# A build-time timetable that learns of the port shared by VectorE and GpSimd, takes its durations from a trace, and may send more elementwise operations to VectorE

## The chip, the core and the metric

The kernel runs on one core of a Trainium2 chip. The core has a matrix engine (PE, TensorE), an engine for elementwise work with two tensor inputs (DVE, VectorE), one for activations with scale and bias (ACT, ScalarE), a general engine (POOL, GpSimd) and a queue that issues DMAs (SP, SyncE). The engines run their own instruction streams in order and wait for each other by semaphores. The metric is the device time of one execution in microseconds (us); lower is better.

## What is computed

Two layers of a diffusion backbone over 512 latent tokens and 256 context tokens, width 1024, all in float32. Layer 0 mixes tokens with gated linear attention (GLA, 4 heads) and differential attention (4 heads) side by side; layer 1 with a bidirectional state-space mixer (SSD, 32 heads in 8 groups of 4). Each layer then runs a SwiGLU feed-forward network (FFN) of hidden width 2816. In short:

```
for layer in range(DEPTH):
    mod_x = jax.nn.silu(c) @ mod_w[layer] + mod_b[layer]          # 6 shifts, scales, gates
    hx = x * (1.0 + scm_x) + shm_x                                 # the same for ctx with mod_c
    if layer % 2 == 0: mix_c, mix_x = even_mixer(hc, hx, ...)      # GLA and differential attention
    else:              mix_c, mix_x = odd_mixer(hc, hx, ...)       # SSD
    x = layer_norm(ALPHA * x + gm_x * mix_x, ln_g[layer, 0], ln_b[layer, 0])
    x = layer_norm(ALPHA * x + gf_x * swiglu(x * (1.0 + scf_x) + shf_x, ...), ln_g[layer, 1], ln_b[layer, 1])
    # ctx goes through the same norms, gates and FFN in layer 0
```

## The kernel before

Activations stay in SBUF, tokens in 6 tiles of 128. Weights stream from HBM into 3 slots (`RAW`, 128x1024). Every float32 product is made of three passes (`mm3`): each operand is split into a rounded high part (`hi`, made by ScalarE as a Copy into an fp32r tile) and a low part (`lo = x - hi`, a two-input subtraction on VectorE or GpSimd). For weights that is `RW<-RAW` and `RW<-RAW,RW` in `issue_loads`; for FFN activations `f<-HB` and `f<-HB,f`; for a layer's normed input `R<-HX,R` (shown by the order of instructions as `R_69`).

The kernel is written as one recording pass. `mm`, `dma`, and the proxies `V`, `S`, `G` (VectorE, ScalarE, GpSimd) do not emit an instruction at once: the class `Timing` gives each one a start in a timetable (`fit`, `room`: the first gap on its engine after its inputs are ready) and `flush` emits them all in the order of those starts. So the timetable's costs decide the order on every engine. Work beside the weight products (softmax steps of differential attention, GLA's recurrences, the SSD tiles, the LayerNorm chains) is written as generators (`Chain`); `pump` lets a chain take its next step between two products when the timetable's PE clock has come to the time at which that step's inputs are ready. So the costs also decide where a chain's matmuls stand among the weight products on PE.

`Timing.either` chooses VectorE or GpSimd for a two-input operation: VectorE, if its end plus a bias (in us, given by the caller) is not later than GpSimd's end. Before, the biases are 0 to 9.5, in GpSimd's favour, and a dozen call sites name GpSimd outright: the rotary products in `diff_proj`, `att`, `la`, the gate and residual of `LN.prep` and `LN.finish`, the sums of `y_tile`, the recurrence product of `recur`, half of `mod_sums`. The power in a normalisation (`ALU.pow` with `mhalf`: `sml<-sml,mhalf`, `LNS<-LNS,mhalf`, `RS<-RS,mhalf`) always runs on GpSimd.

In differential attention a unit (one head, one token tile, 24 in all) is a chain: scores on PE, `TENSOR_REDUCE sml<-PS` for the maximum, `sml` scaled, exponentials on ACT, reciprocal, `HB<-HB,sml` 128x768 to combine the two maps, transposes, values, and a tail whose norm goes through GpSimd's power and ends in `TENSOR_SCALAR HB<-HB,sml` 128x128. In layer 1, `conv_out` (`HB<-HB,CW`, 128x770) makes the convolution and each `y_tile` (32 of them) an output tile. `mod_sums` (layer 1's modulation, made during layer 0's FFN) scales rows of `mod_w` and adds them up.

Names in rows: HB is the large buffer of work units, PS is PSUM, R and HX the mixer's input and its float32 form, RAW and RW weights, f FFN slots, l mixer slots, sml, LNS, RS, DS and CBD small statistics. L104 (L105 after) is the line of `flush` that emits everything, so rows are told apart by their tiles.

## Time and profile before

| what | before |
| --- | --- |
| time, median of 3 runs | 2091.33 us (2087.03 to 2094.28) |
| the profiled execution | 2081.43 us, of which the span of the trace is 2079.5 us |
| PE busy | 1935.3 us (93%) |
| DVE, ACT, POOL busy | 1167.9, 809.5, 1037.8 us (56%, 39%, 50%) |
| chain that ended last | PE 57%, DVE 24%, POOL 6%, ACT 6%, issue 5%, DMA 2% |

Busy time of PE is that of pipelined matmuls whose ends are modelled, so it overstates how full PE is. The chain that ended last is followed back from the last instruction: at each step to what released it, or to the instruction before it on its engine.

### The profile page before, as it was taken

To read this page: it belongs to the slowest core of one execution; us is meant where nothing else is said; L and a number is where in the kernel's file an instruction comes from. 1 tells how busy PE (TensorE), PEld (TensorE's weight loads), DVE (VectorE), ACT (ScalarE), POOL (GpSimd) and SP (SyncE) were. 2 spreads that over 40 slices of the span, in tenths; PEclk is the share of its full clock that TensorE was granted. 3 is DMA by queue.
4 is the path that set the end of the run, shared out by engine and by line. 5 is a ranking of instruction groups with operands and counts; after the bars stand their busy time and mean duration, and the time that the engine had idled before them with its cause. 6 is when DMAs were issued, how large, how long until landed. Compare 5 with 4: busy or idle time off the path is not lost.

```text
span 2079.5 us, 27508 instructions
## 1 busy us (share of the span) xinstructions
PE 1935.3 (93%) x10660; PEld 1655.0 (80%) x10660; DVE 1167.9 (56%) x1660; ACT 809.5 (39%) x1512; POOL 1037.8 (50%) x714
## 2 busy tenths in 40 slices
PE   7988999988899999999998888999999889999997
PEld 4867687866799999999886777888787678888885
DVE  3564535478631424423348998877868883223237
ACT  3523135434524333334235355554545443222232
POOL 2423142335774666657587455541725766333355
PEclk9999899998999999999999999999999999999998
DMA  8443411112243443434422423222233324333331
GB/s 277 122 135 104 132 41 30 43 59 75 70 147 108 123 141 112 142 123 124 150 87 61 130 72 101 92 75 89 82 111 102 111 92 146 108 101 100 103 101 61
DMA packets 233360, 217.43 MB, mean 105 GB/s; under 512 B 18901, under 2 KB 202839, under 8 KB 233231
## 3 DMA queue, kind: packets, MB, share of 16 engines
q1 hardware_dynamic: 233231, 215.69, 33.9%
q8 instruction: 83, 1.36, 0.3%
q14 instruction: 46, 0.38, 0.1%
HBM read 204.94 MB, written 10.72 MB: 104 GB/s over the span
## 4 chain that ended last, share of the span: by engine, by line
PE 57%; DVE 24%; POOL 6%; ACT 6%; issue 5%; DMA 2%; SPq 0%; POOLq 0%; ACTq 0%; DVEq 0%
PE PS L104 57%; DVE HB L104 14%; POOL HB L104 5%; ACT HB L104 4%; DVE RW L104 2%; DVE l L104 2%; DVE sml L104 2%; DVE HX L104 1%; DVE LNS L104 1%; ACT RW L104 1%; DVE R L104 1%; DMA HB<-in_x_dram 0%; DMA HB<-acs_rows 0%; ACT R L104 0%; POOL R L104 0%
## 5 line engine op out<-in xcount | busy, mean ns | idle before, releaser
L104 PE MATMUL PS<-R,RW 128*128 128x384 f32 (+3 forms) x5184 | 989.6, 349 | 10.2 <-DVE R L104 4.2
L104 PEld LDWEIGHTS PS<-R,RW 128*128 128x128 f32 (+1 forms) x5184 | 888.0, 189 | 94.9 <-issue 15.5
L104 POOL TENSOR_TENSOR HB<-HB 128x256 f32<-128x256 f32 (+3 forms) x262 | 441.0, 1694 | 183.3 <-ACT HB L104 105.6
L104 POOL TENSOR_TENSOR RW<-RAW,RW 128x1024 fp32r<-128x1024 f32 (+1 forms) x135 | 340.0, 2525 | 332.4 <-ACT RW L104 325.3
L104 PE MATMUL PS<-RW,f 128*128 128x512 f32 x1320 | 307.1, 392 | 6.1 <-DVE RW L104 4.7
L104 ACT ACTIVATE RW<-RAW 128x1024 fp32r<-128x1024 f32 (+1 forms) x222 | 229.3, 1047 | 213.6 <-issue 100.6
L104 PEld LDWEIGHTS PS<-RW,f 128*128 128x128 f32 x1320 | 248.1, 189 | 60.1 <-DVE RW L104 5.8
L104 ACT ACTIVATE HB<-PS 128x512 f32<-128x512 f32 (+4 forms) x247 | 129.5, 533 | 417.8 <-PE PS L104 408.8
L104 DVE TENSOR_TENSOR HB<-HB,PS 128x384 f32<-128x384 f32 (+2 forms) x68 | 39.7, 584 | 358.4 <-PE PS L104 358.0
L104 DVE TENSOR_TENSOR HB<-PS,HB 128x512 f32<-128x512 f32 (+2 forms) x276 | 160.1, 587 | 143.4 <-PE PS L104 120.6
L104 DVE TENSOR_TENSOR RW<-RAW,RW 128x1024 fp32r<-128x1024 f32 x87 | 167.8, 1931 | 88.4 <-ACT RW L104 86.9
L104 ACT ACTIVATE HB<-HB 128x128 f32<-128x128 f32 (+4 forms) x372 | 160.6, 490 | 138.0 <-DVE HB L104 111.2
L104 PE MATMUL PS<-RW,R 128*128 128x256 f32 (+1 forms) x1440 | 199.0, 296 | 8.5 <-ACT R L104 4.2
L104 PEld LDWEIGHTS PS<-RW,R 128*128 128x128 f32 x1440 | 184.7, 194 | 16.8 <-ACT R L104 4.6
L104 PE MATMUL PS<-HB 128*128 128x128 f32 (+6 forms) x896 | 154.7, 362 | 26.2 <-DVE HB L104 12.5
L104 PE MATMUL PS<-RW,l 128*128 128x512 f32 x576 | 156.0, 417 | 6.3 <-DVE l L104 1.9
L104 PEld LDWEIGHTS PS<-HB 128*128 128x128 f32 (+3 forms) x896 | 106.0, 194 | 60.2 <-issue 23.3
L104 POOL TENSOR_TENSOR f<-HB,f 128x384 fp32r<-128x384 f32 (+2 forms) x63 | 88.8, 1410 | 122.8 <-ACT f L104 122.7
L104 PEld LDWEIGHTS PS<-RW,l 128*128 128x128 f32 x576 | 108.4, 195 | 34.0 <-DVE l L104 2.6
L104 PE MATMUL PS<-ident,HB 128*128 128x128 f32 x480 | 79.7, 295 | 54.4 <-DVE HB L104 36.9
L104 PEld LDWEIGHTS PS<-ident,HB 128*128 128x128 f32 x480 | 57.3, 149 | 85.1 <-DVE HB L104 38.3
L104 DVE SCALAR_TENSOR_TENSOR HB<-HB,CW 128x770 f32<-128x770 f32 (+1 forms) x96 | 104.5, 1088 | 2.8
(145 smaller groups left out, 1471.1 us busy)
## 6 DMA issues: line engine op xcount, KB each, us to landing
RAW<-in_ffn_w_in_dram SPq DMA_DIRECT2D x88, 512.0 KB
HB<-in_mod_w_dram SPq DMA_DIRECT2D x48, 512.0 KB
RAW<-in_ffn_w_out_dram SPq DMA_DIRECT2D x44, 512.0 KB
RAW<-in_ssd_w_in_dram SPq DMA_DIRECT2D x40, 512.0 KB
mod<-in_mod_w_dram SPq DMA_DIRECT2D x72, 256.0 KB
HB<-acs_rows SPq DMA_DIRECT2D x64, 256.0 KB
RAW<-in_ev_w_in_dram SPq DMA_DIRECT2D x20, 512.0 KB
xres<-HB SPq DMA_DIRECT2D x16, 512.0 KB
```

The source lines that it names most:

```text
L104: f(*a, **k)
```

## The change

Three things. First, the timetable's costs: other fixed and per-element numbers for VectorE (V), ScalarE (S) and GpSimd (G), for the power, for scans, and for matmuls. Second, a resource L: an operation that reads two SBUF tensors on VectorE, a VectorE `tensor_scalar` or `tensor_copy` from SBUF, and everything but a memset on GpSimd now also books L, so that the timetable places no two such operations at the same time on the two engines. Third, the choice: the biases are gone, GpSimd is taken only if it would end earlier than VectorE by more than the difference of the two costs, the sites that named GpSimd go through `either`, and in `mod_sums` the second half of the products (an ACT scale and a POOL add each) becomes the fused VectorE operation of the first half.

```
@@ COST and busy
-        "V": (0.069, 1.042e-3, 0.03, 0.06),
-        "S": (0.09, 0.833e-3, 0.06, 0.09),
-        "G": (0.13, 2.12e-3, 0.0, 0.0),
+        "V": (0.15, 1.06e-3, 0.03, 0.06),
+        "S": (0.16, 0.875e-3, 0.08, 0.19),
+        "G": (0.16, 2.14e-3, 0.0, 0.0),
...
-        self.busy = {e: [] for e in "VSGQD"}
+        self.busy = {e: [] for e in "VSGQDL"}
@@ product
-        cost = self.gated(t, cost + 0.0027)
+        cost = self.gated(t, cost)
@@ engine
+                    wide = [x for x, m in zip(aps[1:], sizes[1:]) if x not in out and (m > 1 or n == 1)]
+                    lock = op != "memset" if name == "G" else len(wide) > 1 and self.locks(*wide)
                     if ALU.pow in a:
-                        cost = 0.3 + 0.165 * n
+                        cost = 0.38 + 0.165 * n
...
-                        cost = fixed + 0.66e-3 * n
+                        cost, lock = fixed + 0.64e-3 * n, n > 1
+                    elif op == "tensor_tensor_scan":
+                        cost = fixed + 2.1e-3 * n
...
-                    t = self.fit(name, t, cost)
+                    t = self.fit(name, t, cost, lock)
@@ either
-    def either(self, out, a, b, op, bias=0.0):
+    def locks(self, *ins):
+        return all(x.space != bass.MemoryType.PSUM for x in ins)
+
+    def either(self, out, a, b, op):
...
-        (self.V if end["V"] + bias <= end["G"] else self.G).tensor_tensor(out, a, b, op)
+            end[e] = self.room(e, max(t, self.floor.get(e, 0.0)), cost[e], lock or e == "G") + cost[e]
+        g = end["G"] + cost["G"] - cost["V"] < end["V"]
+        (self.G if g else self.V).tensor_tensor(out, a, b, op)
@@ room and fit (the old room is now gap)
+    def room(self, name, t, cost, lock=False):
+        while True:
+            t0, t = t, self.gap(name, t, cost)[0]
+            if lock:
+                t = self.gap("L", t, cost)[0]
+            if t == t0:
+                return t
@@ mm
-        tm.product(o, (l, r), (max(n, 2 * m) if l.dtype == F32R else 4 * max(n, m)) / 2400.0,
+        tm.product(o, (l, r), max(n, 2 * m) / 2400.0 + 0.0133 if l.dtype == F32R else 4 * max(n, m) / 2400.0 + 0.005,
@@ issue_loads
-            tm.either(lo, r, hf, ALU.subtract, 2.0 if limit < len(plan) else 1 if plan[j][0][0] in ("cv", "z", "sw") else 2)
+            tm.either(lo, r, hf, ALU.subtract)
@@ mod_sums
-                    elif m == 0:
+                    else:
                         V.scalar_tensor_tensor(a, r, c, a, ALU.mult, ALU.add)
-                    else:
-                        S.activation(r, r, AF.Copy, scale=c)
-                        G.tensor_tensor(a, a, r, ALU.add)
@@ LN.prep (LN.finish, gate, gla_mix, diff_proj and start likewise)
-            G.tensor_tensor(y, y, self.gate[1 if t < 2 else 0], ALU.mult)
-            G.tensor_tensor(y, y, xr, ALU.add)
+            tm.either(y, y, self.gate[1 if t < 2 else 0], ALU.mult)
+            tm.either(y, y, xr, ALU.add)
@@ LN.chain and gated
-                tm.either(R0[:, 1, ks, c], hx[:, ks, :], R0f[:, 0, ks, c], ALU.subtract, 0.0 if quick else 9.5)
+                tm.either(R0[:, 1, ks, c], hx[:, ks, :], R0f[:, 0, ks, c], ALU.subtract)
...
-                tm.either(RA[c % 5][:, 1, cs], h, RAf[c % 5][:, 0, cs], ALU.subtract, 6.5)
+                tm.either(RA[c % 5][:, 1, cs], h, RAf[c % 5][:, 0, cs], ALU.subtract)
@@ recur and y_tile
-                G.tensor_tensor(heads(s2), heads(s), dv, ALU.mult)
+                tm.either(heads(s2), heads(s), dv, ALU.mult)
...
-            G.tensor_tensor(tt, tt, yo[:, 0:256], ALU.add)
-            G.tensor_tensor(tt, tt, yo[:, 256:512], ALU.add)
+            tm.either(tt, tt, yo[:, 0:256], ALU.add)
+            tm.either(tt, tt, yo[:, 256:512], ALU.add)
```

What it makes of the built program, counted over all its instructions: the matmuls (9886) and the DMAs stay the same in number. GpSimd goes from 719 to 283 instructions, VectorE from 1654 to 2090, ScalarE from 1410 to 1368 (the 42 scalings of `mod_sums`). The largest kinds:

| operation | on GpSimd, before / after | on VectorE, before / after |
| --- | --- | --- |
| weight low part `RW<-RAW,RW` 128x1024 | 133 / 23 | 87 / 197 |
| `HB<-HB` 128x1024 (LN gates, residuals, gains; `mod_sums`) | 114 / 18 | 0 / 54 |
| `HB<-HB` 128x256 (`y_tile`, `recur`) | 128 / 36 | 0 / 92 |
| `HB<-HB,HX` 128x512 (`y_tile`, rotary) | 35 / 8 | 13 / 40 |
| `HB<-l,DS` 128x256 (`y_tile`) | 32 / 22 | 0 / 10 |
| FFN low parts `f<-HB,f`, all widths | 63 / 0 | 5 / 68 |
| `mod_sums` `HB<-HB,CST` 128x1024 | 0 / 0 | 42 / 84 |

Three places show what the order becomes. The first is GpSimd's queue in differential attention; `sml<-sml,mhalf` is the power of a unit's tail, `RW<-RAW,RW` a weight's low part, the two HB operations the rotary product and sum. Before:

```order
L104 TENSOR_TENSOR sml<-sml,mhalf 128x1 x4
L104 TENSOR_TENSOR RW<-RAW,RW 128x1024
L104 TENSOR_TENSOR HB<-HB,HX 128x512
L104 TENSOR_TENSOR HB<-HB 128x512
L104 TENSOR_TENSOR sml<-sml,mhalf 128x1 x3
L104 TENSOR_TENSOR RW<-RAW,RW 128x1024 x2
L104 TENSOR_TENSOR sml<-sml,mhalf 128x1 x3
L104 TENSOR_TENSOR RW<-RAW,RW 128x1024
```

and now, from GLA's last power to the gates of the first LayerNorm:

```order
L105 TENSOR_TENSOR RW<-RAW,RW 128x1024
L105 TENSOR_TENSOR sml<-sml,mhalf 128x6 x2
L105 TENSOR_TENSOR sml<-sml,mhalf 128x1 x15
L105 TENSOR_TENSOR RW<-RAW,RW 128x1024
L105 TENSOR_TENSOR sml<-sml,mhalf 128x1 x5
L105 TENSOR_TENSOR HB<-HB 128x1024 x2
```

Weights and rotary operations have left the queue; the powers stand almost alone.

The second place is VectorE's queue at the same work: two units of differential attention, with their reduction, reciprocal and combination. It now holds:

```order
L105 SCALAR_TENSOR_TENSOR HB<-HB,sml 128x768
L105 SCALAR_TENSOR_TENSOR l_1_1051<-PS,PRM,l_1_1051 128x128
L105 TENSOR_SCALAR sml<-sml 128x1
L105 STREAM_SHUFFLE HB<-HB 128x512
L105 TENSOR_SCALAR HB<-HB,sml 128x128
L105 TENSOR_TENSOR RW<-RAW,RW 128x1024
L105 TENSOR_TENSOR HB<-HB,HX 128x512 x2
L105 TENSOR_TENSOR HB<-HB 128x512
L105 TENSOR_REDUCE sml<-PS 128x2
L105 TENSOR_SCALAR sml<-sml 128x2
```

A weight's low part and the rotary operations now stand in front of the next unit's reduction.

The third place is VectorE's queue in layer 1, at a `y_tile` with its small statistics (`CBD`, `DS`). Before:

```order
L104 TENSOR_TENSOR HB<-HX,ident 128x128
L104 TENSOR_REDUCE CBD<-HB 128x1
L104 SCALAR_TENSOR_TENSOR DS<-HB,CBD 128x4
L104 TENSOR_TENSOR HB<-PS,HB 128x256
L104 SCALAR_TENSOR_TENSOR l_4_7623<-HB,l_4_7623 128x256
```

and now:

```order
L105 TENSOR_TENSOR HB<-HX,ident 128x128
L105 TENSOR_REDUCE CBD<-HB 128x1
L105 TENSOR_TENSOR HB<-HB,HX 128x512
L105 SCALAR_TENSOR_TENSOR DS<-HB,CBD 128x4
L105 TENSOR_TENSOR HB<-l_2_7579,DS 128x256
L105 TENSOR_TENSOR HB<-HB 128x256 x2
L105 TENSOR_TENSOR HB<-PS,HB 128x256
L105 SCALAR_TENSOR_TENSOR l_4_7581<-HB,l_4_7581 128x256
```

Four operations of the tile that GpSimd did have come over.

## Rows read from the trace of the kernel before

**Rows 1.** The page: span, busy time by engine, chain that ended last.

```profile
span 2079.5 us, 27508 instructions
...
PE 1935.3 (93%) x10660; PEld 1655.0 (80%) x10660; DVE 1167.9 (56%) x1660; ACT 809.5 (39%) x1512; POOL 1037.8 (50%) x714
...
PE 57%; DVE 24%; POOL 6%; ACT 6%; issue 5%; DMA 2%; SPq 0%; POOLq 0%; ACTq 0%; DVEq 0%
```

**Rows 2.** Windows by stage: PE, PEld, DVE, ACT, POOL busy; PE clock; DMA.

```profile
0.00:252.00 252.00, 220.79 (x1450) 167.69 (x1450) 128.97 (x258) 79.54 (x111) 75.13 (x50) 0.95 0.49 157
252.00:556.00 304.00, 271.38 (x1558) 224.39 (x1554) 183.58 (x309) 132.18 (x314) 129.04 (x88) 0.94 0.17 52
556.00:1052.00 496.00, 496.00 (x2679) 465.21 (x2680) 171.98 (x176) 173.74 (x224) 307.30 (x145) 1.00 0.41 126
1052.00:1148.00 96.00, 82.75 (x413) 70.28 (x412) 70.88 (x80) 41.08 (x78) 81.78 (x49) 0.95 0.26 76
1148.00:1714.00 566.00, 513.04 (x2989) 436.24 (x2988) 476.30 (x699) 282.16 (x661) 279.22 (x313) 0.98 0.33 96
1714.00:2020.00 306.00, 306.00 (x1395) 255.29 (x1395) 88.58 (x90) 87.16 (x109) 130.22 (x57) 1.00 0.36 109
2020.00:2079.50 59.50, 45.31 (x188) 35.95 (x186) 47.57 (x51) 13.60 (x17) 35.10 (x17) 0.90 0.21 78
```

**Rows 3.** Timeline of POOL, 1141 to 1166: start, duration, operation, count.

```profile
1141.94 10.73 POOL L104 TENSOR_TENSOR HB<-HB 128x1024 f32<-128x1024 f32 x4
```

**Rows 4.** Timeline of DVE in the same stretch.

```profile
1145.37 5.03 DVE L104 TENSOR_SCALAR l<-l 128x384 f32<-128x384 f32 x2
...
1153.01 1.21 DVE L104 TENSOR_TENSOR RW<-RAW,RW 128x1024 fp32r<-128x1024 f32 x1
1154.14 4.25 DVE L104 SCALAR_TENSOR_TENSOR HB<-HB,CW 128x770 f32<-128x770 f32 x4
...
1164.64 0.36 DVE L104 TENSOR_SCALAR l<-l 128x384 f32<-128x384 f32 x1
```

**Rows 5.** Groups of POOL, shapes apart: busy us, mean ns, idle before.

```profile
L104 POOL TENSOR_TENSOR RW<-RAW,RW 128x1024 fp32r<-128x1024 f32 x133 | 337.5, 2544 | 320.3 <-ACT RW L104 313.2 <-PE PS L104 6.7
L104 POOL TENSOR_TENSOR HB<-HB 128x1024 f32<-128x1024 f32 x114 | 302.2, 2663 | 66.8 <-ACT HB L104 64.9
L104 POOL TENSOR_TENSOR HB<-HB 128x256 f32<-128x256 f32 x128 | 107.2, 850 | 81.1 <-DVE HB L104 48.3 <-ACT HB L104 27.0 <-DVE DS L104 2.7
```

**Rows 6.** Chain shares in 252:556, 1052:1148, 1148:1714 and 2020:2080.

```profile
by line: PE PS L104 40.2%; DVE HB L104 16.5%; DVE sml L104 11.9%; ACT HB L104 9.1%; issue 8.2%; POOL R L104 2.7%; DVE RW L104 2.0%; POOL sml L104 1.6%; DVE LNS L104 1.6%; DVE l L104 1.2%; ACT HX L104 0.9%; POOL LNS L104 0.9%; DVE GB L104 0.
...
by line: POOL HB L104 29.6%; DVE HB L104 20.1%; issue 14.2%; PE PS L104 6.9%; DVE LNS L104 6.6%; DVE RW L104 6.3%; DVE R L104 4.6%; DVE l L104 3.5%; POOL RW L104 2.5%; POOL LNS L104 2.2%; POOL f L104 2.1%; DVE HX L104 1.8%; ACT RW L104 1.1%
...
by line: DVE HB L104 27.2%; PE PS L104 23.1%; POOL HB L104 10.0%; issue 8.0%; DVE l L104 6.2%; ACT HB L104 5.4%; DVE RW L104 4.8%; DVE HX L104 3.6%; ACT RW L104 2.5%; DMA HB<-acs_rows 1.6%; DVE LNS L104 1.1%; DMA RAW<-in_ssd_w_out_dram 0.9%
...
by line: issue 16.2%; DVE RW L104 15.9%; DVE HB L104 11.3%; DVE RAW L104 9.2%; POOL HB L104 9.1%; PE PS L104 8.1%; DVE LNS L104 7.8%; ACT HB L104 6.5%; POOL f L104 3.4%; POOL LNS L104 2.8%; POOLq L1802 1.6%; ACTq L1802 1.2%; ACT f L104 1.1%
```

**Rows 7.** Groups of DVE in 252:556 (differential attention, first LayerNorm).

```profile
L104 DVE TENSOR_SCALAR HB<-HB,sml 128x128 f32<-128x128 f32 x24 | 20.3, 846 | 9.6 <-POOL sml L104 9.5
...
L104 DVE TENSOR_TENSOR RW<-RAW,RW 128x1024 fp32r<-128x1024 f32 x2 | 6.2, 3094 | 0.0
```

**Rows 8.** Timeline 352 to 363, in differential attention.

```profile
352.80 2.41 POOL L104 TENSOR_TENSOR RW<-RAW,RW 128x1024 fp32r<-128x1024 f32 x1 [1.47 <-ACT RW L104]
353.35 1.88 DVE L104 TENSOR_SCALAR sml<-sml 128x2 f32<-128x2 f32 x1
...
361.75 0.29 DVE L104 TENSOR_SCALAR HB<-HB,sml 128x128 f32<-128x128 f32 x1 [1.23 <-POOL sml L104]
```

**Rows 9.** Groups of DVE in 1148:1714 (layer 1).

```profile
L104 DVE SCALAR_TENSOR_TENSOR HB<-HB,CW 128x770 f32<-128x770 f32 x80 | 92.5, 1156 | 2.5
L104 DVE TENSOR_TENSOR RW<-RAW,RW 128x1024 fp32r<-128x1024 f32 x36 | 56.1, 1557 | 15.2 <-ACT RW L104 15.0
L104 DVE TENSOR_TENSOR HB<-PS,HB 128x256 f32<-128x256 f32 x96 | 39.1, 419 | 22.2 <-POOL HB L104 21.5 <-issue 0.4
```

More of the change, by code (lines that the diff above doesn't have):

```diff
@@ L182, in room, with fit @@
         return t, i
-    def fit(self, name, t, cost):
-        t, i = self.room(name, t, cost)
-        self.busy[name].insert(i, (t, t + cost))
+    def room(self, name, t, cost, lock=False):
[5 more added lines that the diff above has]
+                return t
+    def fit(self, name, t, cost, lock=False):
+        t = self.room(name, t, cost, lock)
+        for e in name + "L" * lock:
+            self.busy[e].insert(self.gap(e, t, cost)[1], (t, t + cost))
         return t
@@ L647, in chain @@
                 S.activation(R0[:, 0, ks, c], hx[:, ks, :], AF.Copy)
-                tm.either(R0[:, 1, ks, c], hx[:, ks, :], R0f[:, 0, ks, c], ALU.subtract, 0.0 if quick else 9.5)
+                tm.either(R0[:, 1, ks, c], hx[:, ks, :], R0f[:, 0, ks, c], ALU.subtract)
         def finish(self, t):
             y = self.acc[:, t - self.t0, :]
-            G.tensor_tensor(y, y, self.gb[0], ALU.mult)
-            G.tensor_tensor(y, y, self.gb[1], ALU.add)
+            tm.either(y, y, self.gb[0], ALU.mult)
+            tm.either(y, y, self.gb[1], ALU.add)
             dma(self.dst(t), y)
@@ L774, in mod_quarters @@
                         V.tensor_scalar(y[:, a:b], x[:, a:b], g, c, ALU.mult, ALU.add)
-                    (G, V)[k % 2].tensor_tensor(R0[:, 1, k, :], y, R0f[:, 0, k, :], ALU.subtract)
+                    tm.either(R0[:, 1, k, :], y, R0f[:, 0, k, :], ALU.subtract)
                 quarter[0] = q + 1
@@ L870, in gate @@
             S.activation(ab, ab, AF.Ln, bias=1.0)
-            G.tensor_tensor(la, la, ab, ALU.subtract)
+            tm.either(la, la, ab, ALU.subtract)
             V.tensor_tensor_scan(enb[0:64], smask[0:64], la[0:64], 0.0, ALU.mult, ALU.add)
@@ L944, in gla_mix @@
                 V.copy_predicated(two(at), mk.rearrange("p (g t) c -> p g (t c)", g=2), q)
-            G.tensor_tensor(att, attf, attb, ALU.add)
+            tm.either(att, attf, attb, ALU.add)
             yield kdT, v, pair_free
@@ L987, in gla_mix @@
             S.activation(RA[h][:, 0, :], go, AF.Copy)
-            G.tensor_tensor(RA[h][:, 1, :], go, RAf[h][:, 0, :], ALU.subtract)
+            tm.either(RA[h][:, 1, :], go, RAf[h][:, 0, :], ALU.subtract)
         RC, RS = HX[:, 1, 0:512], HX[:, 1, 512:1024]
@@ L1019, in diff_proj @@
                 V.stream_shuffle(sc[:, 0:512], x, swap)
-                G.tensor_tensor(x, x, RC, ALU.mult)
+                tm.either(x, x, RC, ALU.mult)
                 V.tensor_tensor(sc[:, 0:512], sc[:, 0:512], RS, ALU.mult)
-                G.tensor_tensor(x, x, sc[:, 0:512], ALU.add)
+                tm.either(x, x, sc[:, 0:512], ALU.add)
             marks.add(("qk", h))
@@ L1616, in y_tile @@
                 V.tensor_reduce(cbd, R[:, 0, 0, :], AX.X, ALU.add)
-            tm.either(A, R[:, 1], cb.unsqueeze(1).to_broadcast([P, 4, P]), ALU.mult, 1.25)
+            tm.either(A, R[:, 1], cb.unsqueeze(1).to_broadcast([P, 4, P]), ALU.mult)
             co = DS[:, n % 3, :]
@@ L1630, in y_tile @@
                             tq(t, 3, hg).unsqueeze(3).to_broadcast([P, 2, 4, 64]), ALU.mult)
[L1631 to L1633 removed]
+            tm.either(heads(tt), heads(xs[:, t, :]), co.unsqueeze(2).to_broadcast([P, 4, 64]), ALU.mult)
+            tm.either(tt, tt, yo[:, 0:256], ALU.add)
+            tm.either(tt, tt, yo[:, 256:512], ALU.add)
             V.tensor_tensor(tt, yd, tt, ALU.add)
```

9 lines of the change are left out of this document (4 added, 5 removed).

## The prediction

> **What bounds the kernel now.** I read the page first [rows 1]: PE is busy 93% of the span, but the chain that ended last is PE for only 57%; DVE holds 24% of it and POOL 6%. So other engines set the end in nearly half of the chain, and the question is where. The windows by stage [rows 2] answer it. In the two FFN stretches, 556 to 1052 and 1714 to 2020, PE is busy the whole time at a clock of 1.00: 802 us in which nothing on DVE or POOL can be won as long as PE is fed. The other 1277.5 us are four mixed stages and a tail. PE idles there by 31.2 + 32.6 + 13.3 + 53.0 + 14.2 = 144 us, and its mean clock is 0.90 to 0.98, which says that part of the time is at the lower of its two levels (1.2 instead of 2.4 GHz). In layer 1 (1148 to 1714) DVE is busy 476 of 566 us, 84%: it is the engine nearest to its limit there.
>
> Next the timelines of DVE and POOL over the same microseconds [rows 3, 4]. While POOL does four 1024-wide operations in 10.73 us, two scalings of 384 elements on DVE take 5.03 us, 2.5 each, as long as one POOL operation; the same scaling takes 0.36 us at 1164.64, when POOL has nothing long. A weight's low part takes 1.21 us on DVE at 1153.01, between two stretches of POOL work. In differential attention [rows 8] a scaling of two elements takes 1.88 us, starting 0.55 us after a POOL weight of 2.41 us; both end within 0.02 us of each other. So DVE operations of these kinds stand still until POOL's operation is done: POOL work costs time on DVE as well.
>
> **The prices.** On POOL a weight's low part is 2.54 us, a 1024-wide sum 2.66, a 256-wide one 0.85 [rows 5]. On DVE the first is 1.21 undisturbed [rows 4]; the second has no DVE row, so I take the weight's 1.21 (same size, two inputs from SBUF). The 256-wide one is bounded by 0.42, the row that reads one input from PSUM [rows 9], and by half of POOL's 0.85; they agree. Every moved operation therefore takes about half its time.
>
> **The change part by part.** The new table entries and the port's booking remove no instruction; they only change order and choice. The choice moves 436 operations. The three largest kinds take 110 x 2.54 + 96 x 2.66 + 92 x 0.85 = 613 us from POOL's 1038 and add 206 x 1.21 + 92 x 0.42 = 288 us to DVE. What that is worth is read stage by stage.
>
> Stage 0 to 252: POOL is busy 75 us of 252 and DVE 129 [rows 2], and DMA is at half its share. I take 0 (bounds 0 to 6, a twelfth of POOL's time).
>
> FFN stretches: 0. Layer 0's takes the bulk of the moved weights and all of `mod_sums`. DVE is busy 172 of 496 us there and POOL 307; even if all of POOL's work came over at half price, DVE would hold 172 + 154 + 42 x 1.21 = 377 of 496. PE covers it; without that cover only the 42 new fused operations, some 51 us, would show. The same in layer 1's FFN: 89 + 65 of 306.
>
> Stage 252 to 556, differential attention: the tail's last scaling takes 0.85 us in the mean against 0.29 undisturbed [rows 7, 8]; 24 of them lose 13.4 us, each inside a unit's serial chain. Two DVE weights of 3.09 us lose 3.8 in all, and they are 2.0% of the chain, 6.1 us [rows 6]. `R` on POOL is 2.7% of the chain, 8.2 us, half of which goes: 4.1. The small scalings lose a few us more, up to 1.7 at one place [rows 8]; I take 4. Sum 25. Against it stands what is now queued on DVE: the moved weights and rotary operations stand in front of a unit's reduction, and the reduction's scores bank, the exponentials on ACT and the transposes on PE wait behind them. If one unit in three meets one weight of 1.21, that is 24 / 3 x 1.21 = 10. I take 15 (bounds 0 to 25: from every unit meeting one, which eats 29, to none).
>
> Stage 1052 to 1148, the LayerNorm between FFN and layer 1: POOL's HB, RW and f are 29.6 + 2.5 + 2.1 = 34.2% of the chain [rows 6], 32.8 us. All of it on DVE would save (2.66 - 1.21) / 2.66 = 55%, 18 us. DVE's RW, R and l are 14.4%, 13.8 us; a pair as in [rows 4] gives back more than half, 7 us. But PE idles by only 13.3 us here, with about 5 us of clock (1 - 0.95 over 96). I take 14 (bounds 5 to 25). What is late next is the chain of statistics itself, DVE LNS, 6.6% there.
>
> Stage 1148 to 1714, layer 1. From the counts in the program DVE gains here 92 x 0.42 + 10 x 0.42 of the tiles, 19 products of 512 at twice 0.42 (the 8 others are rotary), and about 8 LayerNorm operations at 1.21: 39 + 4 + 16 + 10 = 69 us. It loses stretch: 80 convolution steps from 1.156 to 1.06, 8 us [rows 9, 4]; 36 weights from 1.557 to 1.21, 12.5 us; the kinds without an undisturbed row I put at as much again times a half, 10. That is 30. DVE then has 476 + 69 - 30 = 515 us of work. How densely can it be filled? Between its present 84% and full I choose 94%, nearer to full since the port's booking keeps standstills out of its time; the stage then takes 548 us, a gain of 18. The chain gives the other view: POOL's HB is 10.0% of it, 57 us, of which 92/128 moves and half is saved, 20 us; DVE's HB, l, RW and HX are 41.8% of it, and that share of the 30 us is 13: 33 at most. I take 18 (bounds -47, at DVE's present 84%, to +33).
>
> Tail, 2020 to 2079.5: DVE's RW and RAW and POOL's HB and f are 15.9 + 9.2 + 9.1 + 3.4 = 37.6%, 22.4 us [rows 6]. With everything at undisturbed prices half, 11, goes, but the work that POOL had at the same time must now be queued in front of the last weights. I take 7 (bounds 0 to 12).
>
> Order on PE: the chains' steps now stand behind other numbers of weight products, since both kinds of step have other prices. No row shows what that is worth; its bounds are the idle time it could fill or open, taken as a third of layer 1's 53 us either way, and nearer to the side of the longer, traced prices: +5 (bounds -18 to +18).
>
> Sum: 0 + 0 + 15 + 14 + 18 + 7 + 5 = 59. The profiled execution took 2081.43 us, span 2079.5 and 1.9 around it, so 2022. It was 0.5% under the median of the runs, 2091.33; at the same ratio the sum gives 2032. I say 2025.
>
> A rule to be weighed against this: layer 1's row shows DVE at 84% [rows 2], and the change gives it more. The Trainium skill (Perfetto Trace Analysis, Optimizing Scalar/DVE Operations) says that work should be offloaded from a saturated DVE to ScalarE or even GpSimd, which is the opposite; by that the 18 of layer 1 becomes the -47 above. The same passage adds that the two share a read port, so that moving work between them may not help; the trace agrees, with 2.5 us for a scaling of 0.36, and by that half the 18 stands.
>
> **The rivals.** (1) VectorE becomes the bound of layer 1. For it: 84% busy now, and in-order, so that each moved sum delays convolution steps that hold PE's next product. Against it: its busy time contains stretch. If it can be filled no denser than now, 515 / 0.84 = 613, 47 us more; if the remaining POOL work stretches it as before, 545 / 0.84 = 649, 83 more. With the other stages' 41 gained the profile goes to 2087 or 2123, 2097 to 2133 on the median's scale; I give 2110. It decides once DVE's fill stays under 515 / (566 + 41) = 85%. (2) The gain is hidden: the freed time in differential attention and LayerNorm is taken by the next wait in line (ACT's exponentials, the statistics), half of each term: 2081.4 - 29 = 2052, or 2062 on the median's scale. (3) Nearly all of the chain's stretch and POOL time is won, and PE's clock with it: the upper bounds 6 + 25 + 25 + 33 + 12 + 18 = 119, 1962, or 1972. (4) The change doesn't do what it says: with its own table GpSimd stays where it is. The counts speak against it (GpSimd 719 to 283); only a balance of gains and losses gives 2091.
>
> **How the numbers follow.** What this kernel's measurement can tell from no change is about 0.3%, 6 us. Chances: my forecast, 1985 to 2055, 0.56; (3), under 1985, 0.12; (2), 2055 to 2085, 0.13; no change, 2085 to 2097, 0.07; (1), above 2097, 0.12. Faster 0.81, same 0.07, slower 0.12. The range runs from 1975, inside (3), to 2095, which leaves out (1): about 0.18 outside.
>
> **What would show it.** Right: POOL busy near 230 to 300 us; the tail's scaling in differential attention near 0.3 to 0.5 us; weights on DVE near 1.3 instead of 1.56 to 3.09; both FFN stretches as long as before; the LayerNorm between FFN and layer 1 without a run of ten POOL operations in the chain; layer 1 near 548 us with DVE above 90%. Wrong: PE idle inside an FFN stretch with DVE as releaser; layer 1 longer than 566 us with DVE in the chain for more than now; weights on DVE still at 1.9 or more.

## The result, and the profile after

The changed kernel takes 2057.51 us (median of 4 runs, 2054.08 to 2060.4), the kernel before beside it 2089.18 us (2082.14 to 2094.28): ratio 0.985, 95% interval 0.9814 to 0.9886. It is faster by 31.7 us, 1.5%, where the prediction had 66 (from 2091.33 to 2025). Of e6 below, one run of 2715.61 us at a clock of 0.65 is left out as a slow one. The profiled execution took 2059.78 us, its span is 2058.1, 21.4 shorter than the span of [rows 1].

The page of the changed kernel: span, busy time, chain that ended last.

```profile
span 2058.1 us, 27239 instructions
...
PE 1925.8 (94%) x10660; PEld 1656.1 (80%) x10660; DVE 1380.8 (67%) x2096; ACT 763.7 (37%) x1470; POOL 230.6 (11%) x278
...
PE 71%; DVE 18%; ACT 3%; issue 3%; DMA 3%; POOL 1%; SPq 0%; POOLq 0%; DVEq 0%; ACTq 0%
```

GpSimd has all but left, and TensorE holds 71% of the chain instead of 57%. To see where the time went, both kernels are cut at the same weight products of TensorE (numbers 812, 1727, 4330, 4700, 6940 and 8333 of the 8520 products that read RW), so that a stage holds the same products in each. Windows of the changed kernel (PE, PEld, DVE, ACT, POOL busy; PE clock; DMA):

```profile
0.00:252.10 252.10, 230.54 (x1531) 178.09 (x1532) 155.89 (x293) 80.42 (x113) 17.24 (x23) 0.97 0.50 159
252.10:523.90 271.80, 248.13 (x1482) 207.25 (x1482) 187.38 (x347) 133.25 (x316) 33.35 (x38) 0.97 0.19 57
523.90:1019.90 496.00, 494.83 (x2673) 463.72 (x2672) 283.96 (x318) 124.69 (x177) 17.77 (x10) 1.00 0.40 127
1019.90:1115.60 95.70, 83.54 (x421) 71.68 (x420) 79.48 (x103) 38.56 (x75) 26.81 (x24) 0.93 0.26 80
1115.60:1696.60 581.00, 519.77 (x2982) 445.34 (x2981) 503.37 (x835) 287.40 (x664) 123.33 (x176) 0.95 0.32 92
1696.60:2002.50 305.90, 305.90 (x1394) 255.18 (x1394) 131.15 (x146) 85.19 (x108) 9.60 (x4) 1.00 0.37 112
2002.50:2058.10 55.60, 43.12 (x188) 34.83 (x186) 39.53 (x59) 14.21 (x18) 2.55 (x4) 0.94 0.18 67
```

The kernel before, cut at the same products, where the cut differs from [rows 2]:

```profile
0.00:267.40 267.40, 236.19 (x1530) 179.13 (x1531) 132.85 (x263) 80.84 (x113) 79.76 (x53) 0.94 0.47 150
267.40:557.90 290.50, 257.88 (x1488) 214.85 (x1487) 180.81 (x305) 132.75 (x316) 126.24 (x85) 0.95 0.18 54
557.90:1052.00 494.10, 494.10 (x2668) 463.31 (x2667) 170.88 (x174) 171.88 (x220) 305.48 (x144) 1.00 0.41 126
1052.00:1149.70 97.70, 84.45 (x421) 71.67 (x420) 72.58 (x80) 41.08 (x78) 83.48 (x49) 0.95 0.27 81
1149.70:1714.10 564.40, 511.44 (x2982) 434.95 (x2981) 474.70 (x700) 282.16 (x661) 277.52 (x313) 0.98 0.33 95
```

Stage by stage: the first stage 15.3 us shorter, differential attention 18.7, FFN 0 longer by 1.9, LayerNorm 2.0 shorter, **layer 1 longer by 16.6**, FFN 1 equal, the tail 3.9 shorter (59.5 before). That is the span's 21.4. The medians differ by 10 more, because the profiled execution of before was one of its quicker ones and the changed kernel's was not.

The operations that the prediction priced, groups of the changed kernel by form (mean ns behind the busy time):

```profile
L105 DVE TENSOR_TENSOR RW<-RAW,RW 128x1024 fp32r<-128x1024 f32 x197 | 249.0, 1279 | 204.4 <-ACT RW L105 203.7
L105 DVE SCALAR_TENSOR_TENSOR HB<-HB,CW 128x770 f32<-128x770 f32 x80 | 94.1, 1176 | 3.3
L105 DVE TENSOR_TENSOR HB<-HB 128x1024 f32<-128x1024 f32 x54 | 74.1, 1400 | 10.1 <-ACT HB L105 9.6
L105 DVE TENSOR_TENSOR HB<-HB 128x256 f32<-128x256 f32 x92 | 50.2, 547 | 3.4
L105 DVE TENSOR_SCALAR HB<-HB,sml 128x128 f32<-128x128 f32 x24 | 8.9, 371 | 8.2 <-POOL sml L105 7.6
```

A weight is at 1.28 us in the mean (1.21 assumed), a 1024-wide sum at 1.40 (1.21), a 256-wide one at 0.55 (0.42). The assumed prices are those of an operation that GpSimd does not disturb, and the trace bears them out: the medians are 1.23, 1.22 and 0.43 us, and the means are above them by some operations that still stood beside a GpSimd one. The tail's scaling fell from 0.85 [rows 7] to 0.37. The mean of the convolution's step did not fall: 1.18 against 1.16 [rows 9], where 1.06 was assumed. Its median is 1.02 us in both traces; 17 of the 80 steps took 1.10 us or more before and 12 take 1.19 or more now, each of them while GpSimd was at work. Four steps that took 4.25 us together without it [rows 4] take 6.49 beside one weight on GpSimd in the changed kernel:

```profile
1409.60 6.49 DVE L105 SCALAR_TENSOR_TENSOR HB<-HB,CW 128x770 f32<-128x770 f32 x4
...
1412.87 2.41 POOL L105 TENSOR_TENSOR RW<-RAW,RW 128x1024 fp32r<-128x1024 f32 x1 [21.85 <-ACT RW L105]
```

In the LayerNorm between FFN 0 and layer 1, the chain of the changed kernel no longer holds POOL HB, 29.6% in [rows 6], and yet little is won; the waits of PE there show what is late instead, one wait of 6.8 us for HX (2.3 us before, one wait):

```profile
by line: PE PS L105 50.2%; DVE HB L105 20.3%; DVE RW L105 9.4%; issue 5.2%; ACT R L105 3.1%; DVE LNS L105 3.0%; DVE R L105 3.0%; ACT RW L105 1.8%; ACT HX L105 1.2%; DVE HX L105 1.2%; POOL LNS L105 1.2%; DVE l L105 0.4%; DVE low L105 0.1%; P
...
PE PS L105 <- DVE HX L105: 7.7, 2, 6.8
```

The timelines of POOL and DVE show why HX comes late. Two weights on DVE take 6.64 us in place of 2.4, since GpSimd does two 1024-wide operations at the same time, and HX stands behind them in DVE's queue:

```profile
1087.77 6.17 POOL L105 TENSOR_TENSOR HB<-HB 128x1024 f32<-128x1024 f32 x2
```

```profile
1088.38 6.64 DVE L105 TENSOR_TENSOR RW<-RAW,RW 128x1024 fp32r<-128x1024 f32 x2
1094.95 0.72 DVE L105 TENSOR_SCALAR HX<-PS,GB 128x128 f32<-128x128 f32 x2
```

The timetable books such operations apart, but on the chip the engines start by their inputs, and here they met.

In layer 1 POOL HB fell from 10.0% of the chain [rows 6] to 0.8%. TensorE's longest waits there (us in total, times, longest) are all for VectorE:

```profile
PE PS L105 <- DVE HB L105: 23.1, 18, 6.0
PE PS L105 <- DVE l L105: 12.1, 8, 5.9
PE PS L105 <- DVE HX L105: 9.2, 5, 4.0
PE PS L105 <- DVE RW L105: 8.3, 3, 5.7
```

Before, the two largest were:

```profile
PE PS L104 <- DVE HB L104: 24.2, 19, 4.5
PE PS L104 <- POOL HB L104: 7.0, 12, 1.3
```

### The profile page after: what moved, and what is told of

Its sections match the earlier page's. It is cut to its first block, busy times and chain, and to the rows that moved or that the text cites. A ratio compares the mean times of both kernels' runs of the same rounds, so it can differ in the third digit from the quotient of the medians.

```text
span 2058.1 us, 27239 instructions
## 1 busy us (share of the span) xinstructions
PE 1925.8 (94%) x10660; PEld 1656.1 (80%) x10660; DVE 1380.8 (67%) x2096; ACT 763.7 (37%) x1470; POOL 230.6 (11%) x278
## 4 chain that ended last, share of the span: by engine, by line
PE 71%; DVE 18%; ACT 3%; issue 3%; DMA 3%; POOL 1%; SPq 0%; POOLq 0%; DVEq 0%; ACTq 0%
PE PS L105 71%; DVE HB L105 12%; DVE RW L105 2%; ACT HB L105 2%; DVE l L105 1%; DMA HB<-acs_rows 1%; DMA HB<-in_x_dram 1%; DVE HX L105 1%; DVE LNS L105 1%; DVE sml L105 1%; ACT RW L105 1%; DMA HB<-in_mod_w_dram 0%; POOL LNS L105 0%; DVE R L105 0%; ACT R L105 0%
## 5 line engine op out<-in xcount | busy, mean ns | idle before, releaser
L105 DVE TENSOR_TENSOR RW<-RAW,RW 128x1024 fp32r<-128x1024 f32 (+1 forms) x198 | 249.4, 1275 | 211.0 <-ACT RW L105 210.3
L105 DVE TENSOR_TENSOR HB<-HB 128x256 f32<-128x256 f32 (+4 forms) x196 | 162.2, 837 | 22.9 <-ACT HB L105 17.8
L105 PE MATMUL PS<-HB 128*128 128x128 f32 (+6 forms) x896 | 148.8, 352 | 10.9 <-DVE HB L105 7.6
L105 POOL TENSOR_TENSOR HB<-HB 128x256 f32<-128x256 f32 (+1 forms) x54 | 73.0, 1364 | 510.6 <-DVE HB L105 362.5
L105 ACT ACTIVATE f<-HB 128x384 fp32r<-128x384 f32 (+2 forms) x68 | 37.4, 550 | 238.3 <-DVE HB L105 238.3
L105 DVE SCALAR_TENSOR_TENSOR HB<-HB,CST 128x1024 f32<-128x1024 f32 x84 | 105.0, 1278 | 0.0
```

Of the source, the lines that this page charges most:

```text
L105: f(*a, **k)
```

## The experiments

Two questions were open: why layer 1 got longer where 18 us were to be won, and where layer 0's 34 us came from, of which the prediction had 15. For the first the theories were: the work moved to VectorE lengthens layer 1 by its amount; layer 1 answers to any change of order, and the changed kernel's own order is an unlucky one; TensorE's lower clock costs the time. For the second: the moved operations, or the order that the new durations give.

The expectations count layer 1 from product 4660: 589.2 us in the changed kernel and 572.6 before, the same loss of 16.6. Where they set the 589 against 566, the 566 belongs to the cut of [rows 2], and the loss comes out 6 us too large. The times of layer 1 below are from product 4700.

The parts of the change are switched apart by four variables (all "new" is the changed kernel, all "old" the one before): `costs` (durations of V, S, G), `choice` (the rule of `either`, its biases and the sites that named GpSimd), `lock` (the port is booked), `mmcost` (prices of products).

**Layer 1 as before, all else changed.**

```diff
+    tm.costs = 'old'; tm.choice = 'old'; tm.lock = False; tm.mmcost = 'old'
     ln, cs = layer1(ln, cs)
```

> Layer 1 alone gets the old timetable and the old choice of engine back; all else is as changed. Theory A (VectorE bounds layer 1: the work moved to it there costs more time than the ended standstills give back): layer 1 falls from 589 us to 566 plus or minus 5, and the whole comes to about 2035 us. Rival B (the stage is not slower by itself: weight products that run ahead by 41 us at its start merely wait there for the same end): layer 1 stays 580 to 590 us and the whole stays at 2055 to 2060.

Measured: 2045.93 us (2043.29 to 2047.09), ratio 0.9797 (0.9774 to 0.9819). The change is better without its part in layer 1, which is as long as before: 561.7 us. Theory A's length of layer 1 came; its time for the whole, which has these 6 us in it, was too short by 11.

**Layer 1 with the old choice but the new durations and the booking.**

```diff
+    tm.choice = 'old'
     ln, cs = layer1(ln, cs)
```

> In layer 1 alone, operations go to GpSimd by the old rules (biases, fixed sites), while the new durations and the booking of the port stay; all else as changed. Theory A (VectorE's moved work bounds layer 1): 560 to 572 us for layer 1, 2030 to 2040 in all. Theory C (the new durations place layer 1's steps badly, whoever does them): layer 1 stays 585 to 595 us and the whole 2055 to 2065.

Measured: 2072.1 us (2069.87 to 2078.98), ratio 0.9932 (0.991 to 0.9955). Layer 1 takes 596.4 us, longer still, although GpSimd has its work back (busy for 279.5 us, 277.5 before). That is theory C's answer, and the whole is above even its range. TensorE's largest wait there:

```profile
PE PS L112 <- POOL HB L112: 34.9, 8, 20.9
```

So the moved work alone is not the cause. Work that stays on GpSimd under the new durations and the booking comes later, and TensorE waits for it.

**The choice alone, and the tables alone, in the whole kernel.**

```diff
-    costs, choice, lock, mmcost = "new", "new", True, "new"
+    costs, choice, lock, mmcost = "old", "new", False, "old"
```

> The old durations without the port's booking, but the new choice of engine everywhere. Theory A: layer 1 near 589 us or longer, since VectorE holds the same work; layer 0 keeps most of its 32 us. Theory C: layer 1 falls to 566 us or less and the whole to about 2035. If the booking and durations are what won layer 0's 32 us, this loses them: 2065 to 2075.

Measured: 2090.23 us (2085.37 to 2093.76), ratio 1.0006 (0.9989 to 1.0023): no change. Layer 1 takes 580.1 us, as long as in the changed kernel, with VectorE busy for 506.4: the moved work does this with the old durations too, as theory A has it. But layer 0 keeps only 5 of its 34 us, where theory A expected most.

```diff
-    costs, choice, lock, mmcost = "new", "new", True, "new"
+    costs, choice, lock, mmcost = "new", "old", True, "new"
```

> New durations and the port's booking everywhere, but the old choice of engine. Theory A: layer 1 at most 566 us, as VectorE has its old work, and layer 0 keeps only what order gives, 0 to 10 of its 32 us: 2070 to 2090. Theory C: layer 1 at 589 us or more, and layer 0's gain kept in part: 2085 to 2110.

Measured: 2139.58 us (2136.23 to 2143.29), ratio 1.0249 (1.0218 to 1.0279). That is above both ranges. It loses 32.5 us in layer 1 (596.9 us), and 19.7 in FFN 0 (513.8 us). In FFN 0 TensorE's one long wait is for a weight on GpSimd:

```profile
PE PS L112 <- POOL RW L112: 14.8, 1, 14.8
```

The parts need each other: 0% and +2.5% apart, -1.5% together.

**Without the booking; with the old prices of products; with the old durations.** Each is the changed kernel with one switch back (`lock` False; `mmcost` "old"; `costs` "old").

> All as changed, but the shared port is not booked. If the booking is what makes the changed timetable right (rival E: knowledge of the port), layer 0's 32 us shrink to 15 or less and the whole comes to 2070 to 2085. If the booking matters little because hardly any work is left on GpSimd, the whole stays 2052 to 2064 and each stage within 5 us.

Measured: 2048.78 us (2045.65 to 2050.54), ratio 0.9816 (0.9781 to 0.9851). That is below both ranges: booking the port gains nothing here. But it also books less than the section on the change says. In `engine` the test `x not in out` drops an input that is also the output, so the convolution's steps and the sums in place (`y_tile`'s) book no L, though the trace shows such steps held by GpSimd. A booking that has them was not run.

> All as changed, but matmuls have their old, shorter prices in the timetable (0.163 instead of 0.173 us for 384 columns). Theory F (layer 0's 32 us come mostly from PE's order, which follows from the matmul prices and the engines' durations): PE's clock in the timetable runs ahead, chains' steps stand in front of other products, and layer 0 loses 10 to 20 of its 32 us; 2065 to 2080. If the matmul prices carry nothing: 2052 to 2064.

Measured: 2049.2 us (2048.1 to 2050.1), ratio 0.9822 (0.977 to 0.9873). That is below both ranges too. Layer 0 keeps 31 of its 34 us, so the prices of products carry little of it; the 8 us less are layer 1's (566.3 us).

> All of the change (port booked, free choice of engine, matmul prices) but the durations of VectorE, ScalarE and GpSimd of before. If layer 0's 32 us come from the order that the new durations give, layer 0 keeps only 5 to 12 us of them, and the time is 2075 to 2095. If they come from the choice that knows of the booked port, layer 0 keeps 25 or more, and the time is 2045 to 2065.

Measured: 2064.16 us (2055.68 to 2066.86), ratio 0.9862 (0.9827 to 0.9897). The time fell into the second theory's range, but by layer 1 (566.9 us); layer 0 kept 13.5 us of its 34, which is close to the first theory's 5 to 12.

Layer 0 in all of these, cut at products 812 and 1727 (windows; PE clock in brackets):

| kernel | to 812 | 812 to 1727 |
| --- | --- | --- |
| before | 267.4 (0.94) | 290.5 (0.95) |
| before, order the same there, two more traces (e14, e12) | 273.9 (0.90), 281.3 (0.88) | 290.4, 290.6 |
| choice alone (e3) | 269.4 (0.91) | 283.4 (0.95) |
| choice and booking, old durations (e11) | 267.8 (0.91) | 276.6 (0.96) |
| durations and booking, old choice (e4) | 258.0 (0.96) | 270.3 (0.98) |
| all but booking (e5) | 258.2 (0.94) | 267.4 (0.96) |
| all but the prices of products (e6) | 250.1 (0.97) | 276.8 (0.97) |
| all (after, and nine traces more with its order) | 250.0 to 255.8 | 271.0 to 274.4 |

The new tables give 20 us of differential attention without moving one operation off GpSimd (POOL is busy 128.75 us there, 126.24 before); the choice alone gives 7. Over all of layer 0 the tables alone give 29.6 of the 34 us, the choice alone 5. So most of layer 0's gain is order, not halved operations. Nor does the gain follow the standstills: the tail's scaling, 0.85 us before, is still at 0.68 in e4 and at 0.51 in e3 (groups of e4, then e3):

```profile
L112 DVE TENSOR_SCALAR HB<-HB,sml 128x128 f32<-128x128 f32 x24 | 16.2, 676 | 10.7 <-POOL sml L112 10.4
```

```profile
L112 DVE TENSOR_SCALAR HB<-HB,sml 128x128 f32<-128x128 f32 x24 | 12.2, 507 | 10.4 <-POOL sml L112 9.7
```

Which step of the order gives the 20 us is not settled. The new order also ends a scatter: the order of before takes 267 to 281 us in its first stage, the new one 250 to 256.

**Another order of the same layer 1.** The durations in layer 1's timetable are multiplied by 1.01, by 0.99, and in the kernel before by 1.01. The work stays as it is, but `either` may settle a few operations otherwise.

```diff
+                    cost *= self.nudge
                     t = self.fit(name, t, cost, lock and self.lock)
...
+    tm.nudge = 1.01
     ln, cs = layer1(ln, cs)
+    tm.nudge = 1.0
```

> All as changed, but every duration of VectorE, ScalarE and GpSimd is 1% longer in the timetable while layer 1 is laid out. Theory D (layer 1 reacts to any change of order, by chance): its 589 us move by more than 5 us, either way. Theory C (the new durations are what is bad for it): 586 to 592 us, and the whole 2054 to 2061.

Measured: 2043.88 us (2040.13 to 2045.51), ratio 0.9792 (0.9757 to 0.9826).

> The same with 1% shorter durations in layer 1. Theory D: layer 1 moves by more than 5 us, and not as the mirror image of the nudge upwards. Theory C: 586 to 592 us, the whole 2054 to 2061.

Measured: 2051.36 us (2046.67 to 2055.13), ratio 0.9829 (0.9791 to 0.9867).

> The kernel before, with the durations of layer 1 in its timetable up by 1% and nothing else. If the layer 1 of before (566 us) is one of many orders alike, it takes 560 to 575 and the kernel 2080 to 2098. If its order was a favourable one by chance or by tuning, layer 1 gets longer by 10 or more: 2100 or over; that would mean that the change does shorten layer 1 on the mean, as forecast.

Measured: 2088.77 us (2081.77 to 2102.53), ratio 1.0009 (0.9979 to 1.004). A hundredth in the table moves the changed kernel's layer 1 by 11 to 18 us, to 562.6 and 569.8; before's goes from 564.4 to 570.3. So theory D holds for both nudges, and the layer 1 of before is one of many orders alike, as the last expectation has it.

**Less and more work on VectorE in layer 1.** e9 leaves out two of the convolution's four multiply-add steps, e17 all four, e18 does two of them twice (the steps k are 1 and 3; none; 0, 0, 1, 3, 4, 4); e10, with the 1.01, gives the first step of each tile to ScalarE.

The first pair of lines is e9's, the second e10's:

```diff
-            for k in (0, 1, 3, 4):
+            for k in (1, 3):
...
-            V.tensor_scalar(cv[:, a:b], pre[:, a:b], w(2), PRM[:, 64 + cc:65 + cc], ALU.mult, ALU.add)
+            S.activation(cv[:, a:b], pre[:, a:b], AF.Identity, bias=PRM[:, 64 + cc:65 + cc], scale=w(2))
```

> The changed kernel, whose layer 1 leaves out two of the five taps of its convolution (two of the four multiply-add steps on each tile: 40 steps fewer on VectorE, about 44 us of its work by their 1.1 us each; that part of the output is not computed). If VectorE's amount of work bounds layer 1 (my first rival of the prediction, and the sum's own 515 / 0.94), layer 1 gets shorter by about as much as VectorE lost, 40 to 50 us: 2008 to 2018 in all. If layer 1 is bound by the order and the latency of chains between the engines, with VectorE's work mostly beside TensorE's, it gets shorter by 15 us at most plus what a new order does by chance (some 10 us): 2035 to 2055.

Measured: 2029.58 us (2026.53 to 2037.67), ratio 0.9699 (0.9665 to 0.9733). It lies between the two ranges.

> The changed kernel with layer 1's durations up by 1% (the 2043.9 of an earlier run), and with the first step of the convolution (one multiply and add on each tile, 20 in all, 0.68 us each) on ScalarE in place of VectorE: 13.7 us of work less on VectorE, ScalarE has room. If VectorE bounds layer 1: 2030. If order and latency do: within the spread of orders, 2038 to 2055.

Measured: 2052.86 us (2051.24 to 2054.06), ratio 0.9814 (0.9786 to 0.9843): within the spread of orders.

> The changed kernel, whose layer 1 leaves out all four multiply-add steps of the convolution (80 steps fewer on VectorE, 88 us of its work; that part of the output is not computed). If VectorE's amount of work sets layer 1's length, the time falls by another 40 us from the two taps' 2029.6: 1985 to 1995. If it is worth a third, by 10 to 18: 2012 to 2020. If another bound lies right below, it stays: 2022 to 2032.

Measured: 2020.11 us (2016.26 to 2022.5), ratio 0.9681 (0.965 to 0.9711): at the edge of the range for a third.

> The changed kernel, whose layer 1 does two of the four multiply-add steps twice (40 steps more on VectorE, 44 us more of its work; that part of the output is another). If VectorE's amount of work sets the length: 2090 to 2105. If it is worth a third: 2060 to 2075.

Measured: 2095.52 us (2090.24 to 2099.21), ratio 1.0034 (1.0014 to 1.0054): the range for VectorE's amount.

The windows of layer 1 (products 4700 to 6940) in e17, e9, e7 and e18, one fence each:

```profile
1118.70:1658.90 540.20, 506.00 (x2982) 435.70 (x2981) 405.67 (x752) 284.32 (x664) 98.74 (x164) 0.97 0.34 100
```

```profile
1120.70:1674.10 553.40, 509.26 (x2981) 438.97 (x2980) 451.70 (x784) 284.41 (x663) 109.23 (x176) 0.97 0.33 96
```

```profile
1119.00:1681.60 562.60, 511.25 (x2981) 438.51 (x2980) 494.01 (x823) 286.21 (x663) 124.38 (x185) 0.97 0.32 95
```

```profile
1114.30:1729.90 615.60, 529.97 (x2981) 449.95 (x2980) 553.27 (x870) 287.26 (x664) 151.13 (x190) 0.93 0.29 87
```

And in all kernels that do layer 1's full work, those with fillers (below) apart:

| layer 1 of | us | DVE busy, us | share | PE clock |
| --- | --- | --- | --- | --- |
| before; nudged (e12); e1 | 564.4; 570.3; 561.7 | 474.7; 477.0; 475.3 | 84%; 84%; 85% | 0.98; 0.97; 0.98 |
| old choice, new tables (e2; e4) | 596.4; 596.9 | 464.9; 466.1 | 78%; 78% | 0.93; 0.93 |
| after | 581.0 | 503.4 | 87% | 0.95 |
| nudged up (e7); down (e8) | 562.6; 569.8 | 494.0; 499.0 | 88%; 88% | 0.97; 0.96 |
| choice alone (e3) | 580.1 | 506.4 | 87% | 0.95 |
| e5; e6; e11 | 561.6; 566.3; 566.9 | 504.1; 498.7; 497.9 | 90%; 88%; 88% | 0.97; 0.97; 0.97 |
| e10 (13.7 us given to ACT) | 571.2 | 484.1 | 85% | 0.97 |

The seven orders with the new choice (after, e3, e5, e6, e7, e8 and e11) have a mean of 570 us, 562 to 581, at some 500 us of VectorE work. From there 53 us more work (e18) make layer 1 46 us longer; 49 us less (e9) make it 16 shorter, the next 46 (e17) 13. Each of the three is one order, and orders of the same work differ by 10 us either way; the steps left out also shorten a tile's chain. With that reserve, VectorE's work sits at a knee: above some 500 us most of it counts, below it a third. The chain that ended last says the same, in e18 and in e17:

```profile
by line: DVE HB L112 41.9%; PE PS L112 26.2%; issue 6.5%; ACT HB L112 6.4%; DVE l L112 4.4%; DVE RW L112 3.9%; DMA HB<-acs_rows 3.3%; DVE HX L112 2.4%; DVE LNS L112 0.9%; POOL HB L112 0.8%; POOL RS L112 0.6%; DMA HB<-xres 0.6%; ACT RW L112 
```

```profile
by line: PE PS L112 72.3%; DVE HB L112 8.2%; issue 4.1%; ACT HB L112 2.9%; DMA HB<-acs_rows 2.4%; DVE RW L112 2.2%; ACT RW L112 1.1%; DMA HB<-xres 1.1%; DVE l L112 0.7%; DVE LNS L112 0.7%; DMA RAW<-in_ffn_w_in_dram 0.7%; DVE DS L112 0.6%; D
```

In no run was VectorE filled by more than 90%. Its longest waits in layer 1 of the changed kernel are for ScalarE and TensorE, the longest before was for GpSimd:

```profile
DVE HB L105 <- ACT HB L105: 29.6, 33, 4.5
DVE HB L105 <- PE PS L105: 13.9, 19, 2.9
```

```profile
DVE HB L104 <- POOL HB L104: 21.7, 41, 1.8
```

**Products that nobody reads, in the places where TensorE waited.** The longest waits stand beside spells at the lower clock, as these windows of the changed kernel show:

```profile
1245.00:1256.00 11.00, 9.35 (x68) 8.52 (x67) 9.76 (x18) 3.49 (x8) 3.57 (x2) 0.99 0.15 39
1256.00:1262.20 6.20, 0.25 (x2) 0.00 (x0) 4.46 (x11) 4.72 (x15) 0.65 (x2) 0.50 0.77 235
1262.20:1266.10 3.90, 3.86 (x14) 3.50 (x15) 2.98 (x6) 1.20 (x4) 0.00 (x0) 0.50 0.51 145
1266.10:1276.00 9.90, 9.39 (x57) 8.09 (x57) 9.43 (x14) 2.38 (x6) 0.23 (x3) 1.00 0.17 54
```

And in every row of the table above layer 1's length times its clock comes to 545 to 556 us, as if the lower clock made up the whole difference. To tell whether the clock costs the time, fillers go ahead of each product that had waited 0.7 us or more in the kernel's own trace, and the plan knows nothing of them:

```diff
+        if self.count in self.FILL:
+            spot = min((self.bank[:, i, 0:P] for i in range(2, 8) if i not in self.held), key=self.free)
+            if self.free(spot) < self.clock - 0.5:
+                for j in range(self.FILL[self.count]):
+                    self.put(self.clock, self.nc.tensor.matmul, (spot, self.one, self.one), ...)
         cost = self.gated(t, cost + 0.0027 * (self.mmcost == 'old'))
```

> The changed kernel with the same order of all its instructions; at the 23 places of layer 1 where TensorE waited 0.7 us or more in its trace, 211 products of two identity matrices stand ahead of the product that waited (as many as fill 0.9 of the wait, into a part of PSUM that nobody reads). If the lower clock costs the time: TensorE waits as long for the other engines, but fewer spells at the lower clock follow; the 35.8 us that layer 1 lost to it fall to 20 or less, and the time to 2035 to 2046. If the waits cost it and the clock only goes along: layer 1 stays within 5 us, or gets longer by fillers that stand in the way: 2053 to 2065.

Measured: 2054.73 us (2052.81 to 2057.38), ratio 0.9851 (0.9806 to 0.9896). Layer 1 and the fillers in it:

```profile
1115.60:1693.90 578.30, 549.70 (x3384) 476.12 (x3383) 501.89 (x832) 285.97 (x662) 123.56 (x176) 0.99 0.32 92
...
L114 PE MATMUL PS<-ident 128*128 128x128 f32 x402 | 48.4, 276 | 0.5 <-DVE HB L114 0.5
```

> The kernel before with the same fillers in its layer 1 (169 products at 27 places, by its own trace). Layer 1 lost only 15.7 us to the lower clock there. If the clock costs the time, it gains 5 to 10 us (2079 to 2085 as median); if the waits do, nothing or a loss.

Measured: 2089.73 us (2072.97 to 2094.8), ratio 0.9999 (0.9967 to 1.0032).

> The changed kernel with layer 1's durations up by 1% (2043.9), with fillers at 44 places of all the mixed stages (332 products). It lost 45.5 us to the lower clock in all. If the clock costs the time, half of that comes back: 2020 to 2032. If not: 2040 to 2055.

Measured: 2040.15 us (2037.4 to 2044.02), ratio 0.9781 (0.9736 to 0.9827).

> The changed kernel with fillers at 44 places of all the mixed stages (365 products). It lost 54.6 us to the lower clock in all. If the clock costs the time, half of that comes back: 2025 to 2037. If not: 2053 to 2068.

Measured: 2049.89 us (2047.78 to 2051.74), ratio 0.9826 (0.9782 to 0.9871). It lies between the two ranges; e13, e14 and e15 lie where the waits cost the time.

The clock rises as meant (layer 1 at 0.99 in e13, at 1.00 in the other three), and the time hardly moves: layer 1 at 581.0 goes to 578.3 and 573.0, at 562.6 to 562.1, at 564.4 to 560.9. In e13 TensorE's own work takes 549.7 - 48.4 = 501 us instead of 519.8, 18 less, and 16 of them come back as waits. The fillers hardly stand in the way: e13 has 201 of them at 21 of the 23 places (two instructions each), and at 20 of these the product behind them still starts only after a gap of 0.1 to 0.8 us. So the clock theory, formed from that product (length times clock), falls for layer 1: the lower clock goes along with the waits and is mostly covered by VectorE. What stays of it is 0.5 to 8 us, and two traces with the same fillers there (e13, e16) already differ by 5.3. On the whole time, by the ratios, it is 0 to 5 us.

## Why the prediction was too large

**The direction and the prices were right, the source of the gain was not.** Moved operations take half their time; POOL is at 230.6 us (230 to 300 foreseen), weights on VectorE at 1.28 (near 1.3), the tail's scaling at 0.37 (0.3 to 0.5), the FFN stretches are 494.1 and 496.0, 305.9 and 305.9, and POOL left the LayerNorm's chain. But 54 of the sum's 59 us were put on the moved operations and on standstills that end, and 5 on order, and the runs show the reverse: the choice alone gains nothing (e3), and layer 0's 34 us come mostly from the order that the durations give. The time lies inside the range by luck in part: the 15 us of the first stage, which the sum had at 0, stand in for some of what layer 1 and the LayerNorm lack. It is also near the second rival's 2062, but not by that rival's mechanism, since differential attention gave more than its term and not half.

**The step that failed is the fill in layer 1**: "Between its present 84% and full I choose 94%, nearer to full since the port's booking keeps standstills out of its time". VectorE's work was foreseen well (515; 503 measured), but the fill is 87%, and at most 90% in any order or amount of work that was run. At 503 us, 87 to 90% gives 559 to 578 us, and before took 564: from 5 us won to 14 lost, not 18 won. The reason given for 94% is not borne out either: without the booking (e5) the fill is 90%, and with it 12 convolution steps are still held. Of the 34.6 us between the forecast gain of 18 and the loss of 16.6, 23.4 are the false fill by the mean of the seven orders (18 and 569.8 - 564.4), and 11.2 are the order that the changed kernel happens to have (581.0 against 569.8); by the two quickest orders (e5 and e7, 562.1) it is 15.7 and 18.9. Which product in that order costs this is not settled; TensorE's waits of 4.0 to 6.0 us above are where to look. Why no order fills VectorE further is not settled either, beyond its waits for ScalarE and TensorE.

The first rival named this place, and its condition held: it decides once the fill stays under 85%, and at 87% layer 1 lost 16.6 us rather than 47, which the rest of the kernel covered. The Trainium skill (Perfetto Trace Analysis, Optimizing Scalar/DVE Operations) says that offloading some work from a saturated VectorE may make sense, which is less than the prediction has it say. On what more VectorE work costs, e18 agrees (46 us for 53); what less work gives is a third (e9 and e17), and e10, with 13.7 us given to ScalarE, has a layer 1 of 571.2 against 562.6 without it, no more than two orders differ.

**Stage 0 to 252, taken as 0 (bounds 0 to 6)**: 15.3 on the profiles, and 21 between the means of the traces of each order (274.2 of three, 253.1 of ten). The step asked only what POOL's own time could hide. It left out that DVE held the chain there too (DVE HB 24.6%, now 9.8%), and TensorE's waits for it. Here too the tables alone have most of it (e4, 258.0). Before and after:

```profile
PE PS L104 <- DVE HB L104: 16.2, 13, 2.5
```

```profile
PE PS L105 <- DVE HB L105: 6.4, 7, 2.1
```

The clock went along (0.94 to 0.97); whether it is a cause here was not tested. The Trainium skill (TensorE: Matmul & The Clock Gate, What's actually happening) says that the number of products run at the lower clock at a kernel's start varies from run to run. The three traces of one order agree for the first stage, with 267.4, 273.9 and 281.3 us at 0.94, 0.90 and 0.88; the last 13 runs of before go from 2078 to 2097 us, and its profile was at the quick end.

**Differential attention, 15**: 18.7 measured. The size was right by luck. The operations did get faster as foreseen, but e4 has all of the gain without moving them and with the tail's scaling at 0.68, and e3, which moves them, has 7.1 us of it.

**LayerNorm, 14 (bounds 5 to 25)**: 2.0, below the bounds. The step that failed is that what POOL and the stretch give up shortens the stage. TensorE idles for 13.3 us before and 12.2 after: the wait for HX took POOL's place, not the statistics. The moved weights stand before HX in VectorE's queue, and the GpSimd work that remains still holds them (6.64 us for two, above), so the stretch that was to go is still there.

**Tail, 7**: 3.9. **Order on PE, +5 (bounds -18 to +18)** was meant as one small term; it is the largest one, with opposite signs: 29.6 us won in layer 0 by the tables alone, and in layer 1 anything from 562 to 581 us for much the same work.
